# Making the second layer's late gates in the projection phase, with seven products in place of eight

## The chip, the cores and the metric

The kernel runs on one core of one Trainium2 chip. The metric is device time in microseconds (us) of one execution, given as the median of several runs. Work inside the core is spread over TensorE (PE, matrix products), VectorE (DVE), ScalarE (ACT), GpSimd (POOL) and the queue of SyncE (SP), which issues nearly all DMAs.

## The reference, cut to what matters

Two layers of an encoder step are computed, for a prompt of 2048 frames and for 64 new frames of a second stream; the width is 1024, in 16 heads of 64.

```
# layer 0 (A)
q, k, v, gate = split(rms_norm(x) @ w_in_a)
x = x + (band_attention(q, k, v, bias) * silu(gate)) @ w_out_a
# shared keys and values, then layer 1 (B)
k, v = split(rms_norm(x) @ w_kv)
q, gate = split(rms_norm(x) @ w_in_b)
x = x + (stick_breaking_attention(q, k, v) * silu(gate)) @ w_out_b
y = rms_norm(x)
```

Everything is float32. The kernel gets its precision from splitting each operand into a high and a low part in the matmul format and adding three products (high·high, high·low, low·high).

## The kernel before

**Four stages in time.** Projections of layer a, attention of layer a, projections of layer b, attention of layer b. Names carry an `_a` or `_b`. Heads go in eight pairs `hp`, each 128 columns wide.

**Projections** (`projections`) work on the tokens in two halves: half 0 is the first 1024 frames and the 64 new ones, half 1 the other 1024 frames. In each half the values `v` are made first (`values`, tile `ps_v`), tile of 128 frames by tile; beside that the normed and turned input is prepared, and `mix` builds sums and differences of input blocks from it on POOL, DVE and ACT, a step at a time, taken from the list `mixing`. Then follow the pairs: `pair` makes one kind (`k`, `q` or `g` for the gate) for two `hp` at once, 256 weight columns by 1024 frames, by seven block products where the plain form has eight. A product (`times`) is 12 matmuls of 512 columns into `ps_x`, `ps_y` or `ps_z`; a pair is 84 matmuls. Around the products a pair readies its own and the next weights: `load` (DMA), `s1`/`s2` (scaling on POOL), `-t1` to `-t4` (differences on POOL), `t1` to `t4` and `b1`/`b2` (splits on ACT and DVE). `this` are the steps of the pair that runs, `following` those of the next and `third` those of the one behind. A slot stands behind each product; in it staged work runs too: `stage_cache` turns cached keys (tile `ks`), `diff_steps` makes differences of value rows (tile `vs`).

**Late jobs.** `DEFER` lists what half 1 of the projections leaves out: in layer b, `g` and `q` of all eight `hp`. These are made as `late_job`s beside the attention: 8 steps a job, 6 plain matmuls of 512 columns a step (`some`, tile `ps_j`), from split weights that half 0 has written to memory (`w_bg`, `w_bq`) and that SP loads back (tiles `lwh`, `lwl`). A gate job ends in a sigmoid on ACT, a product on DVE (tile `sg`) and a store.

**Attention of layer b** is written in beats. A beat makes the scores of one 128-query tile (`z`), turns the weights of an earlier one (`wt`), splits them (`ph` on ACT, `pl` on DVE) and adds two products to `acc`; POOL and DVE make the products along the sticks (`two`, `s`). `ORDER` takes query groups 1 and 0 first for all `hp`, then groups 3 and 2. `RATE["b"]` = 0.3 says how many steps of side work a beat takes from the list `beside`: the late jobs, eight steps that only load the output weights and hold no product, then the output projection (`out_tile`, tile `ps_o`) of the groups that are done. Steps left at the end run by themselves.

**Order.** In the projections and in the side work's first steps the program order holds as written; in attention a scheduler orders each engine's stream ahead of the run. Each engine then executes its own stream in order, and so does SP's queue.

Of the kernel before, what the change touches and what calls it, by code (L numbers as in the profile page):

```python
# [16 lines left out]
P = 128  # L17
# [3 lines left out]
DH = 64  # L21
# [19 lines left out]

DEFER = dict(a=[("k", hp) for hp in range(HP)], b=[(k, hp) for k in "gq" for hp in range(HP)])
KEPT = "b"

RATE = dict(a=0.4, b=0.3)
COLD = 24
# [32 lines left out]
def f32(ap):  # L79
    return ap.bitcast(F32)  # L80
# [45 lines left out]
def encoder_step(ctx: ExitStack, tc: tile.TileContext, a: dict, o: dict):  # L126
# [108 lines left out]

    banks, ends = {}, {}
    done_late = set()
# [32 lines left out]
    def projections(L, x_of, begin, w_v, cv, gv, out_v, jobs, first, prompt, sample, stages):  # L270
        with ExitStack() as own, ExitStack() as beside, ExitStack() as early:
# [251 lines left out]
            def run(does, *names):  # L523
                for x in names:
                    if does:
                        does.pop(x)()
# [9 lines left out]
            def pair(hf, kind, c0, hp, forms, pools, this, following, third, event):  # L536
# [82 lines left out]
                c5 = plain(z)  # L619
                run(this, "t4")  # L620
                run(following, "s2")
                slot(1)
                times(x, mixed(hf, 1), t2, False)
                u2 = plain(x)
                run(this, "t3")
                slot(2)
# [97 lines left out]
            with tc.tile_pool(name=f"v0_{L}", bufs=1) as pool, tc.tile_pool(name=f"v0s_{L}", bufs=1) as vspool:  # L724
# [25 lines left out]
                parted(seq[1], tile1)  # L750
                vws += two_blocks(3, block_rows(0, 3, ring(3)), vw(pool))
                xt[2] = load(seq[2])
                xt[3] = load(seq[3])
                norm(seq[2], xt[2])
                mixing = [x for u in range(4) for x in mix(0, u, [tmp[0], tmp[4 + u], tmp[1], tmp[2]])]
                for i, t in enumerate(seq):
                    leave = values(0, 0, i, t, vws, vspool, vps)
                    if i + 4 < len(seq):
                        xt[i + 4] = load(seq[i + 4])
                    if i + 2 < len(seq):  # L760
                        parted(seq[i + 2], turned(seq[i + 2], xt[i + 2]))
                    if i + 3 < len(seq):
                        norm(seq[i + 3], xt[i + 3])
                    if i < 5:
                        values_beside(i, ("ol", "xr"))
                    if i == 6:
                        raw = [block_rows(1, j, ring(j)) for j in range(4)]
                    if i == len(seq) - 1:
                        vws = [x for j in range(4) for x in two_blocks(j, raw[j], vw(pool))]
                        tick()  # L770
                    leave()
                    if 3 <= i < len(seq) - 1:
                        mixing.pop(0)()
                    if i != len(seq) - 2:
                        tick()
                for i, t in enumerate(seq):
                    values(0, 1, i, t, vws, vspool, vps)()
                    if mixing:
                        mixing.pop(0)()
                    if i == 1:  # L780
# [26 lines left out]
            made += [weights_of(*x, raws[i % 2], forms) for i, x in enumerate(todo[0]) if i]  # L807
            run(made[1], "load", "s1")
            spaces = tc.tile_pool(name=f"s0_{L}", bufs=2, side="right")
# [20 lines left out]
            def turn_ahead(j):  # L830
# [3 lines left out]
                if j == 0:  # L834
                    next_xt[2] = fetched(seq1[2], got["pool"], 2)

            events = {
                last - 1: {
                    1: [begin_next],
# [11 lines left out]
                },  # L851
            }
            all_pairs(0, todo[0], made, forms, (spool, spool), staging, events)
            while waiting:
# [5 lines left out]
            with tc.tile_pool(name=f"v1_{L}", bufs=1) as pool, tc.tile_pool(name=f"v1s_{L}", bufs=1) as vspool:  # L860
# [8 lines left out]
                for i, t in enumerate(seq1):  # L869
# [15 lines left out]
                    if i == 3:  # L885
                        tmp = [opool.tile([P, 2, CH], F32, name="mixed", tag="ol", bufs=2) for _ in range(2)]
                        tmp = [x[:, j] for x in tmp for j in range(2)]
                        mixing = [x for u in (1, 2, 3, 0) for x in mix(1, u, tmp)]
                    if 3 <= i < NK - 1:
                        mixing.pop(0)()  # L890
                    if i != NK - 2:
                        tick()
                for i, t in enumerate(seq1):
                    values(1, 1, i, t, vws, vspool, vps)()
                    for _ in range(1 + (i in (0, 2))):
                        if mixing:
                            mixing.pop(0)()
# [12 lines left out]
                    if i == 5:  # L910
                        run(made[0], "t1")
                        assert not mixing
                    if i == 6:
                        forms[1] = whole_forms("ol")
                        run(made[0], "b2")
                    if i == 7:
                        run(made[0], "-t2", "-t4")
# [11 lines left out]
            staging["pool"] = beside.enter_context(tc.tile_pool(name=f"s1_{L}", bufs=2))  # L929
            run(made[1], "load")  # L930
            all_pairs(1, todo[1], made, forms, (spool, rest), staging, {0: {0: [partial(run, made[1], "s1")]}})
            assert not staged[1]
# [7 lines left out]
    def stage_cache(L, hp, c, pool):  # L940
# [14 lines left out]
        def turn():  # L955
            ps = bank("ps_c")
            for j in range(4):
                flip(ps[:, j * P : j * P + P], kr[:, j])
            ks = pool.tile([P, 2, CH], F32R, name="ks", tag="ks", bufs=1)
            split(ks[:, 0], ks[:, 1], ps)  # L960
            put(L, "k", hp, to, ks, nc.sync.dma_start)

        def rows_of_values():
            vs = pool.tile([P, 4, 2, P], F32R, name="vs", tag="vs", bufs=2)
            for h in range(2):
# [8 lines left out]
    def rows_in(pool, n):  # L974
        return [pool.tile([P, CH], F32, name=f"v{x}", tag=x, bufs=2) for x in ("vr", "vp")[:n]], lambda: pool.tile(
            [P, 2, CH], F32R, name="vs", tag="vs", bufs=2
        )
# [130 lines left out]
    class Sample:  # L1108
# [21 lines left out]

        def keys_values(self, pool, hp, k0, n, bufs):
            kt = pool.tile([P, 2, n], F32R, name="kt", tag="kn" if n == NS else "kt", bufs=2 if n == NS else bufs)
            c = place(k0) if k0 < T else k0
            queue.load(f32(kt), f32(lay[self.L]["k"][hp][:, :, c : c + n]).rearrange("s p t -> p s t"))

            r0, m = (k0 - NS * (self.L == "b"), P) if n == NS else (k0, n)
            return kt, load_v(self.L, pool, hp, r0, m, bufs)

# [512 lines left out]
    with (  # L1651
# [39 lines left out]
        def items():  # L1691
            for part in ORDER:
                for hp in range(HP):
                    c0, vs = max(min(part) - 1, 0), {}
                    keys = rpool.tile([P, 2, SEEN * CH], F32R, name="keys", tag="keys", bufs=2)
                    for g in part:
                        sums = {}
                        for h in range(2):
# [7 lines left out]
                            for c in fresh:  # L1706
                                vs[c] = load_v("a", rpool, hp, c * CH, CH, KV)
                            gt = lazily(partial(load_gate, "a", pool, hp, g * CH))
                            yield item(hp, g, h, q, gt, sums, bias, keys[:, :, max(g - 1 - c0, 0) * CH :], vs)
                        if hp == HP - 1:  # L1710
                            beat.when_summed(partial(summed, g))
                    if part == ORDER[-1]:
                        yield sample_item(hp)
            beat.when_summed(partial(summed, GROUPS))
# [43 lines left out]
        def sample_item(hp):  # L1758
            st, sums = {}, {}

            def one():

                bs = rpool.tile([P, 576], F32, name="bs", tag="bs", bufs=1)
                for h in range(2):
                    queue.load(bs[h * DH : h * DH + DH], biasd[hp][0:DH, h, 0:576])
                q = new.queries(hp)
                st["gt"] = new.gate(pool, hp)
                st["kv"] = [new.keys_values(rpool, hp, T, CH, 1), new.keys_values(rpool, hp, NP, NS, KV)]
                z = psum.tile([P, 2, CH], F32, name="z", tag="z", bufs=2)
# [343 lines left out]
```

## Time and profile before

| | us |
|---|---|
| median of 3 runs | 3230.65 (3226.43 to 3230.69) |
| the profiled execution | 3227.07 |
| its span in the profile | 3225.2 |
| PE, DVE, ACT, POOL busy | 3141.7, 2220.1, 1862.7, 1711.0 |
| projections a / attention a | 0 to 660 / 660 to 1280 |
| projections b / attention b | 1393 to 1984 / 1984 to 3138 |
| output projection alone | 1280 to 1393, 3138 to 3218 |

The stages are read off the times at which their tiles first and last stand in the trace. A matmul of 512 columns shows some 390 ns in the profile, but starts every 230 ns or so, since consecutive ones overlap; counts and starts are the measure of PE's work, not the sum of durations. Where a row of a timeline ends in square brackets, the engine sat idle for so many us before it, until the instruction named there.

### The profile page before, as it was taken

What the parts mean: (1) busy time and instruction counts of PE and PEld (TensorE: products, weight loads), DVE (VectorE), ACT (ScalarE), POOL (GpSimd) and SP (SyncE); (2) the same over time, 40 slices, a digit from 0 to 9 for tenths busy, and PEclk for the clock granted to TensorE, in tenths of its full rate; (3) what the DMA queues carried; (4) which work ended last, traced back from release to release, by engine and by line L of the source; (5) the groups of instructions that cost most, each with busy time, mean ns of one, the idle gap of its engine ahead of it and who ended that gap; (6) DMA issues with size and microseconds to landing.
All of it is one profiled execution on the core that took longest, in us unless ns stands there. A gap on an engine that the chain in (4) does not pass through costs nothing. (4 is left out here: it accounts for less than half of the span.)

```text
span 3225.2 us, 52124 instructions
## 1 busy us (share of the span) xinstructions
PE 3141.7 (97%) x16784; PEld 2620.3 (81%) x16784; DVE 2220.1 (69%) x3938; ACT 1862.7 (58%) x3743; POOL 1711.0 (53%) x2383
## 2 busy tenths in 40 slices
PE   9999999999998999999999999999999999999999
PEld 7887877778887898877888777888888888888877
DVE  5576466567787775257645664888877888888873
ACT  5444444568887776144544544666666666666652
POOL 4455366736665553034534352444477777777761
PEclk9999999999999999999999999999999999999999
DMA  6698457798899994467998777877735576345423
GB/s 224 200 324 291 172 182 266 248 263 233 225 273 243 250 238 135 157 220 248 314 320 312 256 255 252 237 216 207 201 116 148 154 220 183 112 138 142 135 73 121
DMA packets 476975, 685.28 MB, mean 212 GB/s; under 512 B 61169, under 2 KB 258321, under 8 KB 476702
## 3 DMA queue, kind: packets, MB, share of 16 engines
q1 hardware_dynamic: 474398, 673.56, 67.5%
q10 hardware_dynamic: 2304, 8.39, 0.7%
q8 instruction: 134, 2.20, 0.3%
q14 instruction: 139, 1.14, 0.1%
HBM read 423.06 MB, written 258.76 MB: 211 GB/s over the span
## 5 line engine op out<-in xcount | busy, mean ns | idle before, releaser
L115 DVE TENSOR_TENSOR pl<-wt,ph 128x512 fp32r<-128x512 f32 (+1 forms) x864 | 552.2, 655 | 106.7 <-ACT ph L115 102.9
L115 ACT ACTIVATE ph<-wt 128x512 fp32r<-128x512 f32 (+1 forms) x864 | 485.2, 578 | 190.9 <-PE wt L115 178.5
L115 PE MATMUL wt<-ident,s 128*128 128x128 f32 x3472 | 551.6, 274 | 9.3 <-DVE pl L115 6.5
L115 PEld LDWEIGHTS wt<-ident,s 128*128 128x128 f32 x3472 | 417.8, 141 | 83.9 <-DVE pl L115 13.3
L115 ACT ACTIVATE f<-z 128x512 f32<-128x512 f32 (+4 forms) x680 | 355.2, 536 | 192.2 <-PE z L115 130.7
L115 POOL TENSOR_TENSOR s<-f,s 128x256 f32<-128x256 f32 x416 | 360.4, 867 | 102.0 <-DVE s L115 93.9
L115 PE MATMUL acc<-ph,vt 128*128 128x512 f32 (+3 forms) x1088 | 374.6, 379 | 6.3 <-ACT ph L115 3.6
L115 PE MATMUL z<-kt,q 128*128 128x512 f32 (+3 forms) x1280 | 372.7, 378 | 4.4 <-ACT f L115 2.5
L115 PE MATMUL acc<-pl,vt 128*128 128x512 f32 (+3 forms) x1088 | 363.4, 367 | 9.1 <-DVE pl L115 8.5
L115 POOL TENSOR_TENSOR two<-f 128x256 f32<-128x256 f32 x416 | 259.3, 625 | 153.8 <-ACT f L115 142.2
L115 POOL TENSOR_SCALAR s<-s,rc 128x640 f32<-128x640 f32 (+5 forms) x264 | 201.5, 768 | 239.9 <-DVE rc L115 174.1
L115 DVE TENSOR_TENSOR_SCAN s<-two,s,own 128x256 f32<-128x256 f32 x408 | 300.6, 739 | 34.6 <-POOL two L115 33.3
L115 PEld LDWEIGHTS z<-kt,q 128*128 128x128 f32 x1280 | 219.9, 190 | 35.0 <-ACT f L115 9.7
L115 PE MATMUL ps_x<-x_own,t 128*128 128x512 f32 x864 | 225.2, 409 | 10.6 <-ACT t L115 4.8
L115 POOL TENSOR_TENSOR wraw<-wraw 128x512 f32<-128x512 f32 x96 | 137.2, 1437 | 182.9 <-DVE ohl L115 92.6
L115 DVE CUSTOM_DVE_ANT_0 s<-z,bias 128x640 f32<-128x640 f32 (+4 forms) x256 | 184.7, 733 | 70.4 <-PE wt L115 53.4
L115 PEld LDWEIGHTS acc<-pl,vt 128*128 128x128 f32 x1088 | 193.7, 190 | 42.6 <-DVE pl L115 26.5
L115 DVE TENSOR_TENSOR_SCAN s<-f,own 128x128 f32<-128x128 f32 (+4 forms) x264 | 202.7, 789 | 31.3 <-ACT f L115 30.8
L115 PEld LDWEIGHTS acc<-ph,vt 128*128 128x128 f32 x1088 | 196.7, 190 | 29.1 <-ACT ph L115 8.2
L115 ACT ACTIVATE s<-s,mn 128x640 f32<-128x640 f32 (+5 forms) x264 | 200.3, 760 | 24.3 <-DVE mn L115 23.1
L115 PE MATMUL ps_o<-big,oh 128*128 128x512 f32 x544 | 213.7, 393 | 0.0
L115 PE MATMUL ps_o<-bigl,oh 128*128 128x512 f32 x544 | 213.0, 392 | 0.0
(250 smaller groups left out, 7133.1 us busy)
## 6 DMA issues: line engine op xcount, KB each, us to landing
vt<-v_b SPq DMA_DIRECT2D x80, 512.0 KB, 4.9
v_b<-vs SPq DMA_DIRECT2D x64, 512.0 KB, 3.9
q<-q_a SPq DMA_DIRECT2D x128, 256.0 KB, 6.2
q<-q_b SPq DMA_DIRECT2D x128, 256.0 KB, 4.6
vt<-v_a SPq DMA_DIRECT2D x48, 512.0 KB, 8.8
kt<-k_b SPq DMA_DIRECT2D x96, 256.0 KB, 5.6
v_a<-vs SPq DMA_DIRECT2D x40, 512.0 KB, 3.2
keys<-k_a SPq DMA_DIRECT2D x80, 256.0 KB, 7.1
```

The source lines that it names most:

```text
L115: ins = op(*args, **kwargs)
```

## The change

`DEFER["b"]` keeps only `q`. The gates of half 1 are therefore made by four more pairs in the projections (84 matmuls each), and the eight gate jobs of the attention go (48 matmuls each), with the stores and loads of `w_bg`. `RATE["b"]` goes from 0.3 to 0.2. Five smaller edits come along: the first steps of `mix` start one tile later and stop one tile earlier, and double up later; in a pair, `t4` is split behind `t3` in place of ahead of it; in half 0, `s1` of the second pair moves behind the first product of the first pair, and at the start of half 1 `b2`, `-t2` and `-t4` come one tile earlier; staged keys and values share one ring of three buffers (two in half 1) in place of one and two; and in layer a's attention the new frames' bias, queries and cached keys are asked for one item earlier. At the very start, `load` and `norm` of the third tile stand ahead of the last value weights.

```diff
-DEFER = dict(a=[("k", hp) for hp in range(HP)], b=[(k, hp) for k in "gq" for hp in range(HP)])
+DEFER = dict(a=[("k", hp) for hp in range(HP)], b=[("q", hp) for hp in range(HP)])
-RATE = dict(a=0.4, b=0.3)
+RATE = dict(a=0.4, b=0.2)
...
                 c5 = plain(z)
-                run(this, "t4")
                 run(following, "s2")
                 slot(1)
                 times(x, mixed(hf, 1), t2, False)
                 u2 = plain(x)
-                run(this, "t3")
+                run(this, "t3", "t4")
                 slot(2)
...
                 parted(seq[1], tile1)
-                vws += two_blocks(3, block_rows(0, 3, ring(3)), vw(pool))
                 xt[2] = load(seq[2])
+                raw3 = block_rows(0, 3, ring(3))
+                norm(seq[2], xt[2])
+                vws += two_blocks(3, raw3, vw(pool))
                 xt[3] = load(seq[3])
-                norm(seq[2], xt[2])
...
-                    if 3 <= i < len(seq) - 1:
+                    if 4 <= i < len(seq) - 2:
                         mixing.pop(0)()
...
                     values(0, 1, i, t, vws, vspool, vps)()
-                    if mixing:
-                        mixing.pop(0)()
+                    for _ in range(1 + (i in (0, 2))):
+                        if mixing:
+                            mixing.pop(0)()
...
-            run(made[1], "load", "s1")
+            run(made[1], "load")
...
             events = {
+                0: {0: [partial(run, made[1], "s1")]},
...
+            staged_rows[0] = 3
...
-                    if 3 <= i < NK - 1:
+                    if 3 <= i < NK - 2:
                         mixing.pop(0)()
...
-                    for _ in range(1 + (i in (0, 2))):
+                    for _ in range(1 + (i < 3)):
...
                     if i == 5:
-                        run(made[0], "t1")
                         assert not mixing
+                        forms[1] = whole_forms("ol")
+                        run(made[0], "t1", "b2")
                     if i == 6:
-                        forms[1] = whole_forms("ol")
-                        run(made[0], "b2")
-                    if i == 7:
                         run(made[0], "-t2", "-t4")
...
-            ks = pool.tile([P, 2, CH], F32R, name="ks", tag="ks", bufs=1)
+            ks = pool.tile([P, 2, CH], F32R, name="ks", tag="vs", bufs=staged_rows[0])
...
+                            if part == ORDER[-1] and (g, h) == (part[-1], 1):
+                                at_last = sample_item(hp)
...
                     if part == ORDER[-1]:
-                        yield sample_item(hp)
+                        yield at_last
```

In the last edit `sample_item` itself now issues the loads of `bs` and of the queries and cached keys (its `one` did so before).

**What moves on PE.** The first place is the end of half 1 of layer b's projections. In before, the last keys' pair (`ps_x`, `ps_n`) is followed at once by the attention's first late job (`ps_j`) and scores (`z`).

```order
L115 MATMUL ps_x<-big_15672,t_20111 128x512
L115 MATMUL ps_n<-ident,c 128x128 x8
L115 MATMUL ps_j<-big_15672,lwh 128x512
L115 MATMUL ps_j<-bigl_15673,lwh 128x512
L115 MATMUL z<-kt,q 128x128 x2
L115 MATMUL z<-kt,q 128x256 x2
```

In the changed kernel a gates' pair stands behind the keys' last flips: its second product (`x_new` holds `t1` here), third, and so on.

```order
L115 MATMUL ps_x<-big_15668,ohl 128x512
L115 MATMUL ps_n<-ident,c 128x128 x4
L115 MATMUL ps_z<-x_own_15665,x_new 128x512 x12
L115 MATMUL ps_x<-x_own_15665,t_20084 128x512 x12
L115 MATMUL ps_z<-x_own_15666,olh 128x512 x2
L115 MATMUL ps_z<-x_own_15666,oll 128x512
```

Four such pairs now lie between the keys' last pair and the attention.

**What moves on SP.** The second place is the attention of layer b, first `hp`. In before, weights of gate and query jobs alternate in the queue, and finished gates are stored (`gate_b<-sg`).

```order
L152 DMA gate_b_128<-sg 128x512
L115 DMA lwh<-w_bg_141 128x2x512
L115 DMA lwl<-w_bg_141 128x2x512
L152 DMA gate_b_128<-sg 128x512
L159 DMA gt<-gate_b_128 128x512
L115 DMA gf<-in_norm_f 128x1024
```

After the change only query weights are loaded, and the gates of half 1 have been stored by the pairs' `hl` tiles before.

```order
L159 DMA gt<-gate_b_128 128x512
L115 DMA gf<-in_norm_f 128x1024
L159 DMA qs_21368<-q_b_112 64x2x64 x2
L159 DMA qs_21369<-q_b_113 64x2x64
L152 DMA q_b_111<-sp 128x2x512
L159 DMA qs_21369<-q_b_113 64x2x64
L159 DMA gs<-gate_b_128 128x64
L159 DMA gs<-gate_b_129 128x64
L115 DMA lwh<-w_bq_142 128x2x512
```

The loads of `w_bg` and the stores from `sg` are gone from the queue.

**What moves on POOL.** The third place is the first pair of layer b in half 0. In before, the scaling of the second pair's weights (the first `TENSOR_SCALAR` on `bigl_16703`, which is `s1`) stands ahead of the first pair's `-t3` (the single `wraw<-wraw` behind it).

```order
L115 TENSOR_TENSOR wraw<-wraw 128x4x128 x3
L115 TENSOR_SCALAR bigl_16703<-bigl_16703,g_kv 128x256 x4
L115 TENSOR_TENSOR wraw<-wraw 128x4x128
L115 TENSOR_SCALAR bigl_16703<-bigl_16703,g_kv 128x256 x4
L115 TENSOR_TENSOR bigl_16703<-bigl_16703 128x4x128
```

In the changed kernel the four differences stand together, and both scalings follow.

```order
L115 TENSOR_TENSOR wraw<-wraw 128x4x128 x4
L115 TENSOR_SCALAR bigl_16699<-bigl_16699,g_kv 128x256 x8
L115 TENSOR_TENSOR bigl_16699<-bigl_16699 128x4x128
L115 TENSOR_TENSOR vvp<-vvp,vvr 128x512
L115 TENSOR_SCALAR wraw<-wraw,g_kv 128x256 x4
```

The difference that the fourth product needs no longer stands behind the scaling of another pair's weights.

More of the change, by code (lines that the diff above doesn't have):

```diff
@@ L234, in flip @@
         pe.transpose(out, in_, ident[: in_.shape[0], : in_.shape[0]])
-    banks, ends = {}, {}
+    banks, ends, staged_rows = {}, {}, [3]
     done_late = set()
@@ L930, in projections @@
             run(made[1], "load")
+            staged_rows[0] = 2
             all_pairs(1, todo[1], made, forms, (spool, rest), staging, {0: {0: [partial(run, made[1], "s1")]}})
@@ L963, in rows_of_values @@
         def rows_of_values():
-            vs = pool.tile([P, 4, 2, P], F32R, name="vs", tag="vs", bufs=2)
+            vs = pool.tile([P, 4, 2, P], F32R, name="vs", tag="vs", bufs=staged_rows[0])
             for h in range(2):
@@ L1129, in gate, with keys @@
             return gt
-        def keys_values(self, pool, hp, k0, n, bufs):
+        def keys(self, pool, hp, k0, n, bufs):
             kt = pool.tile([P, 2, n], F32R, name="kt", tag="kn" if n == NS else "kt", bufs=2 if n == NS else bufs)
@@ L1134, in keys_values, with rows @@
             queue.load(f32(kt), f32(lay[self.L]["k"][hp][:, :, c : c + n]).rearrange("s p t -> p s t"))
+            return kt
+        def rows(self, pool, hp, k0, n, bufs):
             r0, m = (k0 - NS * (self.L == "b"), P) if n == NS else (k0, n)
-            return kt, load_v(self.L, pool, hp, r0, m, bufs)
+            return load_v(self.L, pool, hp, r0, m, bufs)
+        def keys_values(self, *where):
+            return self.keys(*where), self.rows(*where)
         def scores(self, z, q, kt, stop=True):
@@ L1759, in sample_item @@
             st, sums = {}, {}
+            bs = rpool.tile([P, 576], F32, name="bs", tag="bs", bufs=1)
+            for h in range(2):
+                queue.load(bs[h * DH : h * DH + DH], biasd[hp][0:DH, h, 0:576])
+            q = new.queries(hp)
+            cached = new.keys(rpool, hp, T, CH, 1)
             def one():
[L1763 to L1766, printed above, removed]
                 st["gt"] = new.gate(pool, hp)
-                st["kv"] = [new.keys_values(rpool, hp, T, CH, 1), new.keys_values(rpool, hp, NP, NS, KV)]
+                st["kv"] = [(cached, new.rows(rpool, hp, T, CH, 1)), new.keys_values(rpool, hp, NP, NS, KV)]
                 z = psum.tile([P, 2, CH], F32, name="z", tag="z", bufs=2)
```

2 lines of the change are left out of this document (1 added, 1 removed).

## The prediction, made before the changed kernel ran

> **What bounds the kernel now.** I read the page's first part, then windows over the stages, then the timeline where PE sat idle. The first row is from the page; the next two are windows (length, then busy us of PE, PEld, DVE, ACT and POOL with counts, clock, DMA share, GB/s): attention of layer b as a whole, and the output projection alone at the end.
>
> ```profile
> PE 3141.7 (97%) x16784; PEld 2620.3 (81%) x16784; DVE 2220.1 (69%) x3938; ACT 1862.7 (58%) x3743; POOL 1711.0 (53%) x2383
> sum 1098.00, PE 1081.91 PEld 902.08 DVE 926.17 ACT 729.12 POOL 731.32; mean PE 360.64 PEld 300.69 DVE 308.72 ACT 243.04 POOL 243.77
> 3138.00:3210.00 72.00, 72.00 (x319) 59.62 (x319) 29.65 (x53) 23.29 (x52) 10.87 (x14) 1.00 0.42 136
> ```
>
> PE bounds the kernel: 97% of the span. What can shorten it is fewer matmuls, or fewer of the waits that make up the other 3%. But DVE is busy 926 of 1098 us (84%) in layer b's attention, and the change takes PE work away exactly there. So the question is which of the two is late when PE has less to do. The same kernel shows attention with and without side work. The next windows are in order: group 1 and 0, groups 3 and 2 up to the last side work, and then two stretches without any (first split in two, then split again).
>
> ```profile
> 2013.00:2330.00 317.00, 313.82 (x1867) 266.77 (x1865) 269.15 (x449) 207.54 (x446) 148.52 (x256) 1.00 0.79 217
> 2330.00:3025.00 695.00, 686.55 (x3902) 570.66 (x3902) 579.38 (x927) 459.22 (x911) 514.06 (x949) 1.00 0.51 148
> 2617.00:2671.00 54.00, 51.55 (x310) 42.27 (x309) 48.26 (x80) 40.59 (x81) 42.53 (x82) 1.00 0.97 304
> 3026.00:3112.00 86.00, 81.53 (x472) 64.65 (x471) 77.64 (x125) 62.36 (x127) 68.74 (x130) 1.00 0.33 102
> 2617.00:2641.00 24.00, 24.00 (x157) 20.83 (x156) 21.95 (x39) 19.12 (x39) 18.83 (x35) 1.00 0.96 271
> 2641.00:2671.00 30.00, 27.55 (x155) 21.44 (x154) 26.31 (x41) 21.47 (x43) 23.70 (x48) 1.00 0.97 331
> 3026.00:3050.00 24.00, 23.17 (x149) 19.58 (x148) 22.12 (x39) 18.33 (x40) 17.27 (x32) 1.00 0.72 219
> 3050.00:3112.00 62.00, 58.37 (x324) 45.07 (x323) 55.51 (x87) 44.03 (x88) 51.47 (x99) 1.00 0.18 57
> ```
>
> With side work PE is busy 99% and DVE 83 to 85%. Without it DVE goes to 89 and 90%, and PE begins to wait, though not at once: of the first 24 us it loses nothing in one stretch and 0.83 us in the other; afterwards it loses 2.45 of 30 (8%) and 3.63 of 62 (6%). A burst of side work lets DVE catch up, and that lasts some 24 us.
>
> **Term 1: the gate jobs leave the attention.** The row is the output projection's own matmuls, which follow each other without a wait.
>
> ```profile
> 3138.00:3210.00 72.00, 72.00 (x318) 59.62 (x319) 9.66 (x14) 1.19 (x2) 1.00 0.42 136
> ```
>
> 72.00 / 318 = 0.2264 us a matmul. Eight jobs of 48 are 384 matmuls: 384 x 0.2264 = 86.9 us off PE. Their 16 products on DVE go as well (11.0 us, below), and on SP the loads of `w_bg` and the stores from `sg`; nobody but these jobs waited for them, save at the start (term 4).
>
> **Term 2: four pairs more in half 1.** Layer a makes its gates so already. The first row is the window over seven of its pairs in half 1 (7 x 84 = 588 matmuls; 592 are recorded, with four of the next stage); the second, from the chain of waits, is one product of 12.
>
> ```profile
> 508.50:647.80 139.30, 137.71 (x592) 109.92 (x591) 86.19 (x98) 68.75 (x117) 102.94 (x94) 1.00 0.76 267
> 1928.50 2.80 PE ps_z L115 x12
> ```
>
> 139.30 / 7 = 19.9 us a pair, so 79.6 us; seven bare products, 7 x 2.80 = 19.6, give 78.4, and 80.5 stands for twice the 1.6 us of waiting in that window. The pairs' scaling, differences, splits and stores run beside PE there: DVE is busy 62%, ACT 49%, POOL 74%, DMA 0.76. In layer b the same stage now moves less (row of the keys' pairs), so raw gate weights and gate stores find room.
>
> ```profile
> 1909.50:1977.50 68.00, 67.95 (x319) 55.22 (x320) 37.84 (x47) 35.03 (x60) 31.85 (x31) 1.00 0.68 233
> ```
>
> If PE stays the bound, terms 1 and 2 make 79.6 - 86.9 = -7.3.
>
> **Term 3: side work comes thinner.** The rows are the late jobs' and the output projection's matmuls alone, in three windows of the attention.
>
> ```profile
> 2013.00:2330.00 317.00, 92.08 (x362) 65.31 (x360) 10.99 (x16) 9.57 (x16) 1.00 0.79 217
> 2330.00:2617.00 287.00, 79.29 (x312) 57.95 (x312) 8.26 (x12) 7.21 (x13) 1.00 0.46 135
> 2671.00:3025.00 354.00, 97.76 (x381) 70.25 (x381) 10.22 (x15) 0.00 (x0) 1.00 0.48 135
> ```
>
> Side work runs in bursts of half a job, 24 matmuls; 312 in 287 us is one burst in 22.1 us, of which 24 x 0.2264 = 5.4 us are the burst and 16.7 lie between. A rate of 0.2 for 0.3 makes that 1.5 x 16.7 = 25 us: just where the two stretches begin to lose. What remains, (362 + 312 + 381 - 384) / 24, is 28 bursts. At 0 to 0.83 us each that is 0 to 23 us; I take the mean of the two rows, 0.42, so 11.8, since nothing tells which stretch is the usual one. The two holes without side work grow too: the eight steps without a product last 54 x 1.5 = 81 us, the other perhaps 95; some 36 us more at 7% are 2.5. Term 3 is +14.3, bounds +2.5 and +25.7. It can't be below nothing: PE is busy 24.00 of 24 us at best.
>
> **Term 4: waits that the small edits meet.** Each row ends with PE's idle time and its cause; the ACT and DVE rows are the causes' own waits.
>
> ```profile
> 253.51 3.08 PE L115 MATMUL ps_x<-x_own,t 128*128 128x512 f32 x8 [3.85 <-DVE c L115]
> 251.54 0.60 ACT L115 ACTIVATE ks<-ps_c 128x512 fp32r<-128x512 f32 x1 [7.27 <-DMA k_b<-ks]
> 1524.54 0.47 PE L115 MATMUL ps_f<-ident,nn 64*128 64x64 f32 x2 [2.48 <-DVE nn L115]
> 1522.74 0.63 ACT L115 ACTIVATE t<-wraw 128x512 fp32r<-128x512 f32 x1 [4.66 <-POOL wraw L115]
> 1519.64 1.84 POOL L115 TENSOR_SCALAR bigl<-bigl,g_kv 128x256 f32<-128x256 f32 x4 [9.52 <-DMA bigl<-in_w_kv]
> 1900.69 1.99 PE L115 MATMUL ps_x<-x_own,t 128*128 128x512 f32 x3 [3.44 <-ACT t L115]
> 1450.35 0.50 PE L115 MATMUL ps_v<-vwh,x_own 128*128 128x512 f32 x1 [1.64 <-ACT x_own L115]
> 1452.64 0.79 PE L115 MATMUL ps_v<-vwh,x_own 128*128 128x512 f32 x1 [1.56 <-DVE x_own L115]
> 1844.81 0.49 PE L115 MATMUL ps_v<-vwh,big 128*128 128x512 f32 x1 [0.77 <-ACT vwh L115]
> 1845.99 0.50 PE L115 MATMUL ps_v<-vwl,big 128*128 128x512 f32 x1 [0.69 <-DVE vwl L115]
> 1003.81 1.43 PE L115 MATMUL z<-keys,q 128*128 128x320 f32 x4 [8.04 <-DVE mn L115]
> 1002.99 0.76 DVE L115 CUSTOM_DVE_ANT_0 s<-z,bs 128x576 f32<-128x576 f32 x1 [8.46 <-DMA bs<-bias]
> 1986.42 0.70 PE L115 MATMUL z<-kt,q 128*128 128x128 f32 x4 [1.55 <-DMA kt<-k_b]
> 1988.89 0.79 PE L115 MATMUL ps_j<-big,lwl 128*128 128x512 f32 x1 [1.32 <-DMA lwl<-w_bg]
> ```
>
> - *Shared ring.* ACT waited 7.27 us for the one `ks` buffer and held up what PE needed. With three buffers -3.9; what is late next is DVE's own work, which ran to time there.
> - *`s1` behind the first product.* POOL stood at the second pair's weights for their DMA while ACT wanted `-t3`. POOL's order now has the difference first: -2.5.
> - *`b2`, `-t2` earlier.* ACT's `t` came 3.44 us late at the start of half 1. A tile is 24 matmuls, over 5 us, but ACT and DVE run late there with value rows too: -2.4.
> - *`mix` later and stopped earlier.* The four waits for `x_own` and `vw` sum to 4.66; about half, -2.4, since the steps only move.
> - *New frames' loads.* The wait of 8.04 is for the bias `bs`. Its tile is shared with the late keys' rows, and SP's order has the store of those rows ahead of the load as before; two query loads leave the eight rows between. -1, bound -8.0.
> - *Start of the attention.* The keys were stored four pairs earlier: -1.9 of 2.87.
> - `t4` behind `t3` and the first tile's `norm` go at nothing: both follow the order of need, with ACT and DVE half idle; a wait there would be of the size of the 0.7 us above, either way.
>
> Sum: -14.1, bounds 0 and -25.3 (all six in full).
>
> **The sum.** -86.9 + 79.6 + 14.3 - 14.1 = -7.1. Against the profiled execution, 3227.07 us, that is 3220.0. The median shown is 3.6 us above that execution, so on it 3223.6.
>
> **The rivals.**
>
> *DVE takes over* (slower). Attention's DVE work is 926 us less the gates' products:
>
> ```profile
> L115 DVE TENSOR_TENSOR sg<-ps_j,sg 128x512 f32<-128x512 f32 x16 | 11.0, 690 | 23.9 <-ACT sg L115 22.5 <-DMA o_b<-ot 1.2
> ```
>
> 915 us. My attention of 1098 - 86.9 + 14.3 = 1025 us needs DVE busy 89.3% throughout. The stretches without side work reach 89.4 and 90.3%, but with PE at 95%. On the line between these and the stretches with side work (PE 99%, DVE 84%) the attention lasts 1035 us; at the corner of both, 1017. If DVE stays at 87%, it lasts 1052, gains 46 in place of 73, and the sum is 79.6 - 46 - 14.1 = +19.5: 3250. It decides against the change where DVE stays below 915 / (1098 - 65.5) = 88.6%. For it: the margin of 0.7%. Against it: the full 24 us. Chance 0.20.
>
> *The waits move on.* Two thirds of term 4 return one instruction later: +9.4, hence 3233. For it speaks that in half 1 ACT and DVE are late with value rows whatever the order. Chance 0.29.
>
> *DVE's slack lasts.* Term 3 is next to nothing: 3223.6 - 14.3 = 3209. The stretch with 24.00 of 24 speaks for it, the other against. Chance 0.11.
>
> *PE has room.* If PE's share overstated its load, fewer matmuls would not shorten the attention: 79.6 - 14.1, hence 3296. The output projection alone, where nothing but matmuls runs, has PEld busy 59.62 of 72 (83%), and attention 902 of 1098 (82%): as full as a bare stream. Chance 0.01. The Trainium skill ("Perfetto Trace Analysis", "Identifying the Most-Contended Engine") holds matmul busy time a poor measure and wants the share of weight loads read; its 81% here would look like a fifth to spare, and the row of the bare stream says that it is not.
>
> **The numbers.** My own case has the remaining 0.39 and stands at 3223.6, just beyond the 0.2% (6.5 us) that a measurement of this kernel can tell. With DVE's lasting slack, faster has 0.39 + 0.11 = 0.50; same is 0.29; slower 0.20 + 0.01 = 0.21. The range takes in most of both sides: down to 3206 (term 3 at its lower bound and some more of term 4), up to 3243 (halfway into DVE's case). The likeliest case alone spans 3212 to 3228.
>
> **What would show it.** In the new profile: 384 `ps_j` matmuls fewer, attention of layer b some 1025 us long with DVE near 89% and PE near 97%; half 1 of the projections 79 to 81 us longer; no wait for `k_b<-ks` behind PE, none for `nn` in the first pair. It is wrong if attention stays above 1035 us with DVE no higher than 87%, if a new wait of several us stands in the added pairs, or if the six waits come back under other names.

## The result and the profile after

| | before | changed kernel |
|---|---|---|
| median of 3 runs, us | 3230.65 (3226.43 to 3230.69) | 3264.58 (3263.95 to 3265.62) |
| span of the profiled execution, us | 3225.2 | 3263.8 |

The ratio is 1.0113, with an interval of 1.0099 to 1.0127: slower by 34 us. The prediction said 3223.6, with a range to 3243.

Where the 38.6 us of the span lie is read off the first and the last rows of layer b's attention. From the PE timelines: in before it starts at 1986.42 (row shown with the prediction), and its last product on the weights is this:

```profile
3112.71 0.39 PE L115 MATMUL acc<-pl,vt 128*128 128x512 f32 x1
```

In the changed kernel the same two instructions stand here:

```profile
2065.80 0.70 PE L115 MATMUL z<-kt,q 128*128 128x128 f32 x4 [2.54 <-issue]
...
3151.25 0.39 PE L115 MATMUL acc<-pl,vt 128*128 128x512 f32 x1
```

The attention starts 79.4 us later (terms 2 and 4 together; predicted 79.6 less 14.1) and ends 38.5 us later. So it is 40.8 us shorter, where 87 us of PE work (the estimate of term 1) left it and a shortening by 73 was forecast.

The added pairs cost about what was forecast. The window over the last keys' pairs and all four gates' pairs of the changed kernel shows PE without a gap (length, then PE, PEld, DVE, ACT, POOL with counts, clock, DMA share, GB/s):

```profile
1909.00:2062.00 153.00, 153.00 (x701) 124.49 (x700) 69.46 (x88) 70.74 (x119) 75.66 (x79) 1.00 0.51 177
```

What the engines do in the attention: windows over the changed kernel, in the same columns, first groups 1 and 0, then groups 3 and 2 up to the last side work, then the stretch without any, and the sum of a single window over 2090 to 3150.

```profile
2095.00:2430.00 335.00, 324.02 (x1936) 272.14 (x1935) 294.49 (x491) 226.38 (x483) 175.81 (x307) 1.00 0.74 203
2430.00:3060.00 630.00, 606.51 (x3423) 492.33 (x3422) 535.27 (x860) 418.64 (x849) 479.29 (x884) 0.99 0.50 141
3065.00:3150.00 85.00, 80.25 (x463) 63.08 (x462) 76.72 (x125) 60.90 (x124) 70.60 (x134) 1.00 0.38 108
sum 1060.00, PE 1020.78 PEld 835.67 DVE 911.48 ACT 711.75 POOL 731.90; mean PE 1020.78 PEld 835.67 DVE 911.48 ACT 711.75 POOL 731.90
```

PE is busy 96.3% and DVE 86.0%. Neither looks late, yet the stage is 46 us longer than its lost work says. The weight loads show it better. Before, PEld was busy 902.08 of 1098 us (82.2%), now 835.67 of 1060 (78.8%). At the old share the same loads would take 835.67 / 0.822 = 1017 us, so an estimate of the loss is 43 us; by PE's own share (98.5% before) it would be 24. A matmul that shows 390 ns and is followed 230 ns later covers up to 160 ns of a wait, and many waits here are that short. The Trainium skill ("Perfetto Trace Analysis", "Identifying the Most-Contended Engine") wants the weight loads read because pipelined matmuls look smaller in the trace. This trace agrees in part: the level of 81% said nothing of headroom, since a bare stream shows 83%, but the fall of the share comes near the loss.

The waits that are long enough to be listed (what PE waited for: us in total, times, longest), in before's attention and in that of the changed kernel:

```profile
PE acc L115 <- DVE pl L115: 7.8, 24, 0.8
PE z L115 <- ACT f L115: 2.5, 8, 0.8
```

```profile
PE acc L115 <- DVE pl L115: 21.9, 63, 1.2
PE z L115 <- ACT f L115: 8.7, 11, 4.9
```

Nearly three times as many waits for DVE's low parts, and one single long wait for ACT. The weight loads (PEld), one ahead of each matmul, show the short waits too, though a load can also wait while the matmul ahead of it still runs, so that not all of it is lost. First before, then the changed kernel, from the first scores to the last product:

```profile
PEld acc L115 <- DVE pl L115: 22.9, 45, 1.1
PEld z L115 <- ACT f L115: 9.7, 23, 1.2
PEld acc L115 <- ACT ph L115: 5.4, 16, 0.8
```

```profile
PEld acc L115 <- DVE pl L115: 49.5, 83, 1.5
PEld z L115 <- ACT f L115: 26.3, 55, 5.2
PEld acc L115 <- ACT ph L115: 13.0, 45, 0.7
```

So PE waits longer for ACT as well. Adding up in both traces the time from each start of a matmul to the next tells where the loss stands: 28.4 us ahead of products with `pl`, 8.0 ahead of scores (`z`) and 7.8 ahead of turned weights (`wt`), 44 of the 46. That is where PE waits; it doesn't tell which engine is late by itself.

The long wait's place, in the changed kernel's timeline of all engines (ACTq is what issues DMAs on ACT):

```profile
2485.32 0.33 ACTq L115 DMA_DIRECT2D big<-wo  x1
2486.35 4.53 SPq L159 DMA_DIRECT2D vt<-v_b  x2
2489.29 0.33 ACTq L115 DMA_DIRECT2D bigl<-wo  x1
2489.72 0.60 ACT L115 ACTIVATE f<-z 128x512 f32<-128x512 f32 x1 [6.19 <-DMA vt<-v_b]
2490.36 2.26 PE L115 MATMUL z<-kt,q 128*128 128x512 f32 x4 [4.88 <-ACT f L115]
```

These are two of the 16 loads of output weights that ACT issues. From 2485.65 to 2489.29 ACT gets no further than its next DMA issue (two issues of SP at that time take 4.53 us together), the sigmoid behind it is late, and PE stands still for 4.88 us. What held the issue up is not shown. The windows around it show a second price, in the clock column:

```profile
2485.00:2490.00 5.00, 0.49 (x3) 0.18 (x2) 0.56 (x1) 0.28 (x1) 0.00 (x0) 1.00 1.10 191
2490.00:2494.00 4.00, 3.63 (x13) 2.80 (x13) 3.59 (x7) 3.58 (x9) 1.80 (x4) 0.53 1.06 333
2494.00:2498.00 4.00, 4.00 (x22) 3.71 (x21) 2.41 (x6) 1.37 (x3) 4.00 (x6) 0.62 1.06 359
```

For 8 us after the stop the granted clock is 0.53 and 0.62: another 4 x 0.47 + 4 x 0.38 = 3.4 us. The stop and what follows cost 8.3 us.

The small edits: PE's rows in the changed kernel at the places that term 4 named (the shared ring's, near 250, shows no wait any more), with one that term 4 didn't name, at 503.50, where before has 1.16 us.

```profile
503.50 1.11 PE L115 MATMUL ps_x<-x_own,t 128*128 128x512 f32 x2 [3.33 <-ACT t L115]
...
1003.85 1.43 PE L115 MATMUL z<-keys,q 128*128 128x320 f32 x4 [8.23 <-DVE mn L115]
...
1455.82 0.68 PE L115 MATMUL ps_v<-vwh,x_own 128*128 128x512 f32 x1 [2.11 <-ACT vwh L115]
...
1513.67 0.96 PE L115 MATMUL ps_z<-big,bigl 128*128 128x512 f32 x2 [2.38 <-ACT bigl L115]
...
1902.27 1.22 PE L115 MATMUL ps_x<-x_own,t 128*128 128x512 f32 x2 [4.94 <-ACT t L115]
...
2068.44 0.79 PE L115 MATMUL ps_j<-big,lwl 128*128 128x512 f32 x1 [1.94 <-DMA lwl<-w_bq]
```

Apart from the ring's, nearly every wait has come back, some under another name. The first pair of layer b no longer waits 2.48 us for `nn` but 2.38 for `bigl`, which its second product needs. The start of half 1 waits 4.94 us in place of 3.44. The new frames' 8.04 is 8.23. The start of the attention waits 2.54 and 1.94 in place of 1.55 and 1.32.

### The profile page after: what moved, and what is told of

The parts are those of the page before. It is cut to its first block, busy times and chain, and to the rows that moved or that the text cites. A ratio compares the mean times of both kernels' runs of the same rounds, so it can differ in the third digit from the quotient of the medians.

```text
span 3263.8 us, 52063 instructions
## 1 busy us (share of the span) xinstructions
PE 3155.2 (97%) x16736; PEld 2616.8 (80%) x16736; DVE 2244.9 (69%) x3958; ACT 1877.1 (58%) x3779; POOL 1751.5 (54%) x2431
## 5 line engine op out<-in xcount | busy, mean ns | idle before, releaser
L115 PEld LDWEIGHTS wt<-ident,s 128*128 128x128 f32 x3472 | 417.9, 141 | 84.9 <-DVE pl L115 10.5
L115 POOL TENSOR_TENSOR wraw<-wraw 128x512 f32<-128x512 f32 x112 | 162.0, 1456 | 223.6 <-DVE ohl L115 125.4
L115 PE MATMUL ps_x<-x_own,t 128*128 128x512 f32 x960 | 244.1, 403 | 8.7 <-ACT t L115 8.3
L115 PEld LDWEIGHTS ps_x<-x_own,t 128*128 128x128 f32 x960 | 179.3, 190 | 53.4 <-ACT t L115 9.1
L115 POOL TENSOR_TENSOR rstd<-ms,nhalf 128x1 f32<-128x1 f32 (+1 forms) x51 | 35.8, 702 | 332.5 <-DVE ms L115 321.9
```

Source lines behind the costliest of these rows:

```text
L115: ins = op(*args, **kwargs)
```

## The experiments

Each kernel's time is given beside that of the kernel before on the same chip, as a ratio with its 95% interval. "Over before" is the difference of the medians; the changed kernel stands at +33.9 us by that measure.

### Is the loss in the two tables or in the small edits?

`core` is before with the two tables alone:

```diff
-DEFER = dict(a=[("k", hp) for hp in range(HP)], b=[(k, hp) for k in "gq" for hp in range(HP)])
+DEFER = dict(a=[("k", hp) for hp in range(HP)], b=[("q", hp) for hp in range(HP)])
-RATE = dict(a=0.4, b=0.3)
+RATE = dict(a=0.4, b=0.2)
```

> The kernel before with the two tables alone: gates made in half 1, side work at 0.2 steps a beat, none of the small edits. Theory A (with less side work the attention is no longer paced by PE, and hands back some 46 us of the 87): half 1 +79, attention 41 shorter, so 3269 us (+1.2%). Rival B (the small edits reorder the attention or the stages before it, and the loss is theirs): the two tables alone cost terms 1 to 3 as predicted, +7, so about 3238.

Measured: 3263.28 us, 1.0109 (1.0095 to 1.0123), +34.9. The whole loss is there. The attention of `core` starts at 2064.23, 77.8 us later than before: that is term 2 without the small edits.

`small` is the changed kernel with these two lines taken back.

> The small edits alone: gates of layer b stay late and the rate stays 0.3. Theory A (every wait that they removed came back at a neighbour): 3228 to 3233 us, no change. Rival B (they harm by themselves, up to 30 us): 3245 or more. The prediction's term 4 would give 3216.

Measured: 3227.73 us, 0.9999 (0.9990 to 1.0008). The small edits have no effect in sum, though one of them has one. `ring` is before with the shared staged ring alone:

```diff
-            ks = pool.tile([P, 2, CH], F32R, name="ks", tag="ks", bufs=1)
+            ks = pool.tile([P, 2, CH], F32R, name="ks", tag="vs", bufs=staged_rows[0])
...
-            vs = pool.tile([P, 4, 2, P], F32R, name="vs", tag="vs", bufs=2)
+            vs = pool.tile([P, 4, 2, P], F32R, name="vs", tag="vs", bufs=staged_rows[0])
```

> The kernel before with the shared staged ring alone. The prediction's term 4 takes 3.9 us for it (the 7.27 us wait of ACT for k_b<-ks goes): 3224.5. If the wait returns behind it, 3228 as before.

Measured: 3222.39 us, 0.9980 (0.9972 to 0.9989), -6.2. So the ring's wait was a real one, and by these two runs the others together cost about as much as it gains. They were not run one by one.

### Does the amount of side work count, or its spacing?

`thin` is the kernel before with shorter late gate jobs.

```diff
-                mm(ps, wh[:, k], x2[0][:, k, cols], start=(k == 0), stop=False)
+                thin = L == "b" and kind == "g"
+                mm(ps, wh[:, k], x2[0][:, k, cols], start=(k == 0), stop=(thin and k == NK - 1))
+                if thin:
+                    continue
```

> The kernel before, in which the eight late gate jobs of layer b make only the first of their three precision products: 256 of 384 matmuls are left out, and nothing else moves (loads, sigmoids, stores, steps and the rate stay). PE loses 256 x 0.2264 = 58 us of work. If PE paced the attention throughout: 58 us shorter, 3173. Theory A (the attention keeps about half of what PE is spared, as 41 of 87 in the changed kernel): 27 to 30 shorter, about 3202.

Measured: 3196.15 us, 0.9900 (0.9887 to 0.9914), -32.3: of 58 us taken off PE, 26 are lost. The bursts stood as many beats apart as before, only shorter, and nothing was added to the projections. So distance between bursts is not the only thing that costs; their length counts. Part of the 26 is again a long wait, this time for `ph`; the waits of PE in its attention have this row:

```profile
PE acc L115 <- ACT ph L115: 4.9, 6, 3.8
```

`after_r3` takes the changed kernel's side work at the old rate.

```diff
-RATE = dict(a=0.4, b=0.2)
+RATE = dict(a=0.4, b=0.3)
```

> The changed kernel with side work taken at 0.3 steps a beat as before: bursts of 24 matmuls as close as before, but used up earlier, so that the end of the attention runs without any. If the thinner bursts themselves cost (the theory of term 3), the stretch with side work runs at the old pace and the loss moves to a longer bare end: 3250 to 3260 us. If the pace follows the sum of side work wherever it stands, 3264 within 4. If what counts is that no stretch is bare for long, it is worse than 3264, some 3275.

Measured: 3275.20 us, 1.0143 (1.0128 to 1.0159), +46.8. That looks like the price of a long bare stretch, but the windows of this kernel around two stops of PE say otherwise:

```profile
2366.00:2371.00 5.00, 0.19 (x2) 0.00 (x0) 0.16 (x2) 0.25 (x1) 0.93 (x2) 0.97 1.05 279
2371.00:2375.00 4.00, 3.69 (x11) 2.67 (x11) 3.73 (x6) 3.48 (x9) 0.61 (x1) 0.50 1.06 285
...
2389.00:2397.00 8.00, 0.66 (x2) 0.29 (x1) 0.61 (x2) 1.24 (x3) 1.75 (x5) 0.50 1.07 292
2397.00:2400.00 3.00, 3.00 (x11) 2.39 (x11) 2.48 (x5) 1.59 (x4) 1.46 (x2) 0.50 1.03 254
```

While the output weights are loaded PE stands still twice, for some 5 and 7 us, with half the clock behind each. The changed kernel has one such stop. The second one, 7.3 us and the slow clock behind it (3 x 0.5 = 1.5 in the last row), is some 9 of the 13 us between the two kernels. Why they come is open: it is not that the loads stand close, for before issues the same 16 loads within 34 us (2633.2 to 2667.2), this kernel within 49 (2354.0 to 2402.5), and in before's attention PE waits at most 0.8 us for ACT's `f`. So the run says nothing against spreading and nothing for it.

`even` spreads the changed kernel's side work more evenly over the attention.

```diff
-RATE = dict(a=0.4, b=0.2)
+RATE = dict(a=0.4, b=0.18)
...
-        beat = Beat(LAG["b"], HOLD["b"], False, 1.0)
+        beat = Beat(LAG["b"], HOLD["b"], False, 0.6)
```

> The changed kernel with the same side work spread more evenly: a step that only loads output weights counts 0.6 of a step in place of 1, and the rate is 0.18 in place of 0.2, so that the two bare stretches (90 and 103 us) shrink and the bursts stand a tenth further apart. If spacing costs (bare stretches above all, as the step from rate 0.2 to 0.3 with its 11 us suggests): 3250 to 3258. If the loss follows the amount of side work wherever it stands: 3264 within 4. If the denser loads of the output weights hold up ACT's queue: 3268 to 3272.

Measured: 3263.37 us, 1.0109 (1.0093 to 1.0124), +35.3. A tenth more spacing changes nothing, which fits a loss that follows the amount of side work, as in `thin`. One thing did change: in its profiled execution (3271.14 us, the longest of its four) PE's waits for `f` hold no long stop.

```profile
PE z L115 <- ACT f L115: 6.0, 13, 0.9
```

Yet the kernel is no faster. Where the gain went is not shown.

### Which engine needs that side work?

Latency first. `hold3` and `lag6` give the chain behind and ahead of the turned weights one beat more.

```diff
-HOLD = dict(a=1, b=2)
+HOLD = dict(a=1, b=3)
```

> The changed kernel with products of weights and values held back one beat more (3 for 2). Theory A1 (DVE's throughput paces the attention where side work is thin): more distance gives DVE no time, 3264 us within 4. Theory A2 (latency: the chain turned weights, ACT's split, DVE's split, product is spaced in beats, and beats became shorter): the 22 us that PE waits for pl shrink to a few, some 3240 to 3248.

Measured: 3271.77 us, 1.0130 (1.0117 to 1.0143), +43.2. The list of PE's waits shows why it doesn't help:

```profile
PE wt L115 <- DVE pl L115: 23.2, 67, 1.5
PE z L115 <- ACT f L115: 9.6, 12, 5.7
```

The 21.9 us that products waited for `pl` are now 23.2 us that the next turning waits for `pl`, which frees its bank. `pl` is late at whatever needs it next. This speaks for lack of time on an engine and against lack of distance, though neither theory named a time as long as this one.

```diff
-LAG = dict(a=3, b=5)
+LAG = dict(a=3, b=6)
```

> The changed kernel with six beats in place of five between a tile's scores and the turning of its weights. Theory A1: 3264 us within 4. Theory A2, if the late link is the part ahead of the turning (sigmoid on ACT, products on POOL, scan on DVE): 3245 to 3255; if the late link is behind the turning, no change. With 12 buffers for these tiles it can also lose, some 3270, where scores would have to wait for a buffer.

Measured: 3264.44 us, 1.0110 (1.0097 to 1.0123), +35.9. No change either.

`relief` takes work off DVE in the changed kernel.

```diff
-            split(st[0][:, :n], st[1][:, :n], wt[:, :n])
+            m = n // 2
+            act.activation(st[0][:, :n], wt[:, :n], AF.Copy)
+            dve.tensor_tensor(st[1][:, :m], wt[:, :m], f32(st[0])[:, :m], ALU.subtract)
...
-                        st[s][:, at : at + m],
+                        w,
```

Here `w` is `ph` for the first product as before, and for the second the short `pl`, read twice; the low parts of the other half are left out.

> The changed kernel, but in layer b's attention DVE makes only the first half of each low part pl, and the second product takes that half twice (so the low parts of the other half are left out); PE's matmuls, ACT, POOL and the order of dependencies stay. DVE is spared about half of 332 us, some 150. Theory A1 (DVE's throughput): the attention falls to what PE needs, 1011 us and some waits, 30 to 40 shorter, 3225 to 3235. Theory A2 (latency in beats): the chain is 0.3 us shorter per beat out of some 2.5, so perhaps 10 shorter, 3254.

Measured: 3253.80 us, 1.0079 (1.0066 to 1.0092), +25.2: only 8.7 us less than the changed kernel. Yet DVE was spared much; the group of `pl` (count, busy us, mean ns) in the attention of the changed kernel, then of this one:

```profile
L115 DVE TENSOR_TENSOR pl<-wt,ph 128x512 fp32r<-128x512 f32 (+1 forms) x569 | 354.5, 645 | 49.1 <-ACT ph L115 46.9
L115 DVE TENSOR_TENSOR pl<-wt,ph 128x256 fp32r<-128x256 f32 (+1 forms) x572 | 221.8, 398 | 98.4 <-ACT ph L115 91.2
```

That is 133 us of busy time less. The time is the one that theory A2 gave, not A1: a shorter `pl` also shortens the chain, so this run by itself doesn't part lack of time from lateness along the chain, and `hold3` and `lag6` spoke against the second. `relief_before` is the same edit in the kernel before.

> The kernel before with the same edit as relief (in layer b's attention DVE makes half of each low part pl, which is used twice; the other half's low parts are left out). If DVE is late only where side work is thin: 0 to 4 us shorter, 3225 to 3229. If its lateness costs the same with all the side work there: 11 shorter, 3218.

Measured: 3224.43 us, 0.9989 (0.9980 to 0.9998), -3.6. DVE's lateness costs a little there as well, by the medians less than half as much; the interval reaches from -6.5 to -0.6.

`carry_act` moves the copy of one column per full tile from POOL to ACT in the changed kernel.

```diff
-                gps.tensor_copy(to[:, CH : CH + 1], carry)
+                act.activation(to[:, CH : CH + 1], carry, AF.Copy)
```

> The changed kernel with the copy of one column per full tile (the carry, 375 copies of 0.196 us on POOL, 73 us) on ACT, which is busy 67%. Theory E (in the stretches of full tiles POOL, 1.69 us of work a tile, is as near the pace of 1.62 us as PE): 10 to 25 us shorter than the changed kernel's 3264. Theory A1 (DVE alone): 3264 within 4. If ACT becomes late by it: 3270 to 3280.

Measured: 3264.90 us, 1.0110 (1.0097 to 1.0124), +34.9: nothing, where theory E gave 10 to 25. `carry_act_relief` has both.

> carry_act with DVE relieved as in relief (the low parts pl made for half the columns and used twice, so the other half's are left out). Theory E (DVE in diagonal tiles, POOL in full ones): more than both alone, 25 to 40 us shorter than 3264, some 3228 to 3238. If neither engine paces: as relief, 3254 within 4.

Measured: 3245.19 us, 1.0053 (1.0041 to 1.0066), +15.2, that is 18.7 us less than the changed kernel. The relief of POOL that was worth nothing alone is worth 10 once DVE is relieved; the sum lies between the two forecasts. The waits of the weight loads in this attention:

```profile
PEld acc L115 <- DVE pl L115: 26.0, 66, 1.3
PEld z L115 <- ACT f L115: 23.7, 56, 5.0
PEld acc L115 <- ACT ph L115: 13.0, 50, 0.5
```

The waits for `pl` are down from 49.5 us to 26.0, near the 22.9 of before. Those for ACT's `f` and `ph` have hardly moved, 36.7 us where before has 15.1, one long stop of 5.0 among them. So the two reliefs, of DVE and of POOL behind it, return some 19 of the 46 us. Not all of that is of the change, since DVE's relief gained 3.6 in before too; a larger relief was not tried. The waits that are left are mostly for ACT's outputs. Whether ACT is late by itself no run tests: its sigmoid waits in turn for POOL's and DVE's `s`, 69.8 us in the changed kernel's attention for 38.8 in before.

### A bank more, and an accident

Four kernels were to tell whether a PSUM bank more would loosen the chain. To free one, the constant `own` of the scans was moved to SBUF (`own_sb`, the control), and the bank then given to side work (`side`), to the turned weights (`wt4`) or to the scores (`z3`).

```diff
-        own = psum.tile([P, CH], F32, name="own")
+        own = wpool.tile([P, CH], F32, name="own")
...
-        KV, SB = 5, 12
+        KV, SB = 5, 11
```

> Control for the next three: the changed kernel with the constant of the scans (own, 128 x 512) in SBUF in place of a PSUM bank, and 11 buffers for the products along the sticks in place of 12, which makes the room. One PSUM bank is free and unused. If the place of the constant is indifferent to DVE: 3264 us within 4; if DVE's scans get slower by a tenth, some 3300.

> own_sb with the free PSUM bank given to side work (ps_j, ps_o), which so far takes one of the three banks through which the weights are turned (wt). Theory C (PE waits for pl because three banks of wt are too few, above all while side work holds one): the PE waits for DVE's pl shrink, 15 to 30 us less than own_sb. Theory A1 (DVE's throughput): own_sb within 4.

> own_sb with the free bank as a fourth of the ring in which the weights are turned and side work is summed. Theory C: as side, 15 to 30 us less than own_sb. Theory A1: own_sb within 4.

> own_sb with the free bank as a third bank for scores (z) in place of two: PE can run one tile further ahead of ACT's sigmoid. If the waits of z for f and what follows from them pace the thin stretches (theory D: the front of the chain), 10 to 20 us less than own_sb. Theories A1 and C: own_sb within 4.

Measured: `own_sb` 3392.78 us, 1.0506 (1.0492 to 1.0521); `side` 1.0564 (1.0550 to 1.0579); `wt4` 1.0607 (1.0593 to 1.0622); `z3` 1.0449 (1.0435 to 1.0464). The control itself is 129 us slower than the changed kernel, outside both of its forecasts, so the other three tell little: with DVE that late, a bank more for side work or turned weights costs 18 and 32 us, and one for scores gains 20, as theory D gave, but on this slowed kernel. What the control changed are these groups of its attention (count, busy us, mean ns):

```profile
L115 DVE TENSOR_TENSOR_SCAN s<-two,s,own 128x256 f32<-128x256 f32 x401 | 415.3, 1040 | 53.0 <-POOL two L115 49.1 <-PE wt L115 2.8
L115 POOL TENSOR_TENSOR two<-f 128x256 f32<-128x256 f32 x409 | 336.6, 826 | 110.1 <-ACT f L115 99.6 <-DVE s L115 9.4 <-DMA q<-q_b 0.7
L115 POOL COPY s<-s 128x1 f32<-128x1 f32 x401 | 132.1, 331 | 41.8 <-DVE s L115 20.3 <-PE wt L115 20.2 <-PE z L115 1.3
```

The same groups in the changed kernel:

```profile
L115 DVE TENSOR_TENSOR_SCAN s<-two,s,own 128x256 f32<-128x256 f32 x405 | 296.3, 737 | 45.8 <-POOL two L115 44.5
L115 POOL TENSOR_TENSOR two<-f 128x256 f32<-128x256 f32 x413 | 257.9, 627 | 145.8 <-ACT f L115 140.9 <-DVE s L115 4.3
L115 POOL COPY s<-s 128x1 f32<-128x1 f32 x404 | 78.1, 195 | 25.9 <-DVE s L115 20.6 <-PE wt L115 5.2
```

DVE and POOL both got slower: the scan by 41%, POOL's products by 32%, its copies by 70%. The scans alone add some 120 us to DVE, POOL's two groups some 80 and 55. The kernel pays 129. The control has one buffer fewer for the products along the sticks as well, which was not run by itself.

### A version faster than both

`ring_carry` is before with the shared ring and the copy on ACT; `ring_carry_core` adds the two tables.

> The kernel before with the shared staged ring and the carry's copy on ACT; gates late and rate 0.3 as before. The ring alone gave 3222. Theory E: side work covers POOL there, so the copy brings little, 3217 to 3223. If POOL's tail costs there too: 3210.

> ring_carry with the two tables of the change (gates in half 1, rate 0.2). Theory E: the thin stretches gain what carry_act gained over the changed kernel, so 3235 to 3250; only if the thin stretches become PE's again does it reach the 3214 that the change was worth on paper. Theory A1: 3258.

Measured: `ring_carry` 3219.48 us, 0.9972 (0.9960 to 0.9983), -10.5: faster than both kernels. Most of it is the ring; that the copy adds to it is not shown, since the intervals overlap (`ring` had 0.9980). `ring_carry_core` 3261.52 us, 1.0104 (1.0088 to 1.0119), +31.6: the two tables cost 42 us there too, and theory E's 3235 to 3250 did not come.

## Why the prediction was wrong

- **Terms 1 and 2** held. Half 1 with the start of the attention grew by 77.8 us in `core` (79.6 forecast for the four pairs), PE ran without a gap in the added pairs, and the 384 matmuls are gone.
- **Term 3 is the step that failed**: "At 0 to 0.83 us each that is 0 to 23 us", sum +14.3. It measured 46 (86.9 less 40.8). The idea behind it was that a burst lets DVE catch up and that this lasts some 24 us, so that only the distance between bursts costs. `thin` lost 26 of 58 us with the bursts no more beats apart, and `even` won nothing by spreading them a tenth. In place of a reserve of 24 us the traces show waits for `pl`, `f` and `ph` throughout the attention: the reading that fits them, though no run isolates it, is that side work is time in which the other engines need not keep pace. The two rows of 24 us that showed PE busy 24.00 and 23.17 were read from matmul busy time, which hides waits under 160 ns; their weight loads, 20.83 and 19.58 of 24, were not compared with the bare stream's 83%, and the second (82%) already lay below the 87% of the first.
- What the 46 consist of: by their place on PE, 28.4 ahead of products with `pl`, 8.0 ahead of scores and 7.8 ahead of turned weights. By cause less is known. Relieving DVE and POOL together returned about 19. The stop behind ACT's DMA issue with its slow clock is 8.3, which no row of before announced; but `even` is without it and no faster. The rest are short waits, in the weight loads mostly for ACT's `f` and `ph`, and what makes these late stays open.
- **Term 4 failed as a sum**: -14.1 forecast, `small` measured 0. The ring's part was right in kind (-6.2 for -3.9, which lies within the interval of -9.0 to -3.6). For the others a step moved earlier was taken as time gained, without asking what it was moved in front of. The clearest case is `b2`, `-t2` at the start of half 1. First before, then the changed kernel:

```profile
1898.03 4.94 POOL L115 TENSOR_TENSOR wraw<-wraw 128x512 f32<-128x512 f32 x3 [12.15 <-DVE oll L115]
1897.80 0.68 DVE L115 TENSOR_TENSOR vps<-vps,vn 128x512 f32<-128x512 f32 x1
1898.52 0.63 ACT L115 ACTIVATE vs<-vps 128x512 fp32r<-128x512 f32 x1 [1.89 <-DVE vps L115]
```

```profile
1896.25 4.94 POOL L115 TENSOR_TENSOR wraw<-wraw 128x512 f32<-128x512 f32 x3 [8.94 <-DVE oll L115]
1898.32 1.75 DVE L115 TENSOR_TENSOR vps<-vps,vn 128x512 f32<-128x512 f32 x1
1900.10 0.63 ACT L115 ACTIVATE vs<-vps 128x512 fp32r<-128x512 f32 x1 [2.24 <-DVE vps L115]
```

  POOL's differences did come 1.8 us earlier. But on ACT `t` stands behind the value rows `vs`, and these came 1.6 us later: DVE's `vps` for them started 0.5 us later and took 1.75 us in place of 0.68, now beside POOL's differences. So PE waits 4.94 us for `t` in place of 3.44.

- **The rivals.** "The waits move on" and "DVE takes over" both came true. The first was priced at 3233 and happened in full; the second at 3250, with the attention 46 us shorter and DVE at 87% (40.8 and 86.0% came out). They were given as alternatives, each with the other's term left as forecast, though nothing made them exclude each other. Together they give 79.6 - 46 = +33.6, and the range of 3206 to 3243 left that sum out. That the medians show just +33.9 is in part luck: in the two profiled executions it is 79.4 - 40.8 = 38.6. The second's mechanism was too simple, though: with 133 us taken off DVE only 8.7 came back.
- **"PE has room"** was dismissed rightly: 41 us did leave the attention. But the sign to watch was chosen badly: "PE near 97%" came out at 96.3% in an attention that was 32 us longer than forecast.

## What to carry to other kernels

Taking away work that fills one engine, beside a loop in which others are nearly as busy, need not return its whole time: here of each microsecond taken away only about half came back, and that price is had by shortening the filler alone, before anything is moved. In this case the fall of TensorE's weight-load share against a stretch where it is full gave the loss (43 of 46 us) better than matmul busy time did (24). And rivals that can be true together are to be added, not weighed against each other.

## What the runs showed of the hardware

- **A short stop costs twice.** After PE stood still for 4.88 us the granted clock was 0.53 and 0.62 for 8 us, after the two stops of `after_r3` 0.50. Shorter waits did it too: behind the 2.38 us at 1513.67, and at the start of the changed kernel's attention, with waits of 2.54 and 1.94 us close together:

```profile
1514.00:1518.00 4.00, 3.45 (x9) 2.25 (x8) 3.30 (x4) 1.14 (x3) 2.25 (x2) 0.50 0.60 201
...
2066.00:2070.00 4.00, 2.06 (x8) 1.56 (x8) 0.00 (x0) 0.00 (x0) 0.00 (x0) 0.62 1.07 400
2070.00:2074.00 4.00, 4.00 (x12) 3.08 (x11) 0.66 (x3) 0.84 (x2) 0.66 (x2) 0.53 1.08 304
```

  The Trainium skill ("TensorE: Matmul & The Clock Gate", "Part 1: The HAM clock gate (the "warmup" mystery)") states that the clock falls to half after an idle window of about 3.4 us. The stop of 4.88 us agrees; the waits of 2.38, 2.54 and 1.94 us are shorter than that window and the clock fell all the same, and there the measurement decides.
- **The scans' constant operand in SBUF, in place of PSUM, slowed DVE and POOL alike**: 737 to 1040 ns for the scan and 627 to 826 ns for POOL's products. The Trainium skill ("SBUF — State Buffer", "Who interferes with whom") says that a DVE instruction with two SBUF inputs contends with a GpSimd instruction that reads SBUF. The run agrees in that both engines got slower.
- **A DMA issue on ACT can go with a stop of ACT's arithmetic**: 6.19 us without an activation while two loads of 512 KB were to be issued, in a window with a DMA share of 1.10. The other 14 such loads of that kernel came without a stop like it.
